# Hybrid SSD and S5 decoder block: S5 blocks in three parts with half projections between them, TensorE issued there in the written order

## The chip, the core and the metric

The kernel runs on one core of one Trainium2 chip. The metric is the device time of one execution in microseconds (us). The other cores do nothing. The inputs are float32, with a sequence of 512 tokens, 16 learned tokens ahead of it (528 in all) and a model width of 1024.

## What is computed

The reference, cut to what the change touches. The normalised input goes through one projection, whose columns are the gate `z`, the SSD input `xbc`, the step `dt` and the S5 input `u`. The S5 half is 64 groups of 16 channels, each with a complex state of 64 that runs over the whole sequence:

```python
proj = n @ w_in[layer]
z = proj[..., :o_xbc]
xbc = jax.nn.silu(_causal_depthwise_conv(proj[..., o_xbc:o_dt], conv_w[layer], conv_b[layer]))
u = proj[..., o_u:]
...
bu_re = jnp.einsum('blgh,gph->blgp', u, bb_re)
bu_im = jnp.einsum('blgh,gph->blgp', u, bb_im)
...
_, _, s_re, s_im = lax.associative_scan(combine, (a_re, a_im, bu_re, bu_im), axis=1)
y = (jnp.einsum('blgp,ghp->blgh', s_re, c_re.astype(f32))
     - jnp.einsum('blgp,ghp->blgh', s_im, c_im.astype(f32))
     + u * d_skip.astype(f32))
```

Behind that come a GLU on the S5 output, the chunked SSD on `xbc` with the gate `z`, the output projection and an MLP.

## The kernel before

Every large product is made of float32r parts: a weight is split into `whi` and `wlo` (lines 106 to 123), the input into `xhi` and `xlo`, and `mm_cols` (line 139) issues three matmuls for each of 8 slices of the contraction, 24 in all. The projection is made tile by tile of 128 columns. First come the 8 tiles of `u` (bank `pu`), which go to DRAM for the S5 blocks. The 12 tiles of `xbc` (bank `pxb`) are each made in two halves of 264 tokens, so there are 24 half projections of 24 matmuls; line 695 copies each out with ScalarE. The 8 tiles of `z` (bank `pz`) are made in one piece of 512 tokens, 24 matmuls each.

The S5 work is done in 8 blocks of 8 groups by `s5_block(b)`. In the order of its code a block has three parts, which the text calls A, B and C:

- A: VectorE makes powers of the state matrix (`qa`, `qb` at line 504, then `WB` and `CC` at line 509; there is one `WB` and there are two `CC`, used in turn). TensorE transposes `WB` (bank `pb`, line 519, two banks that ScalarE copies into `btr` and `bti`) and multiplies it with `CC` (bank `pk`, line 528). VectorE adds the skip term (line 530), and from `pk` the lag matrix `Tp` is laid out, by ScalarE copies for block 0 (line 535) and through DRAM for the others. ScalarE and VectorE make the cosine and sine tables `co` and `si` (lines 545 to 556; the second shows as `sni` in the profile).
- B: TensorE makes four banks `px` from `btr`, `bti` and the input `ub` (line 570). VectorE reads them in twelve instructions (lines 572 to 577), runs two scans (line 581) and six more instructions that give `sr` and, last, `si` (line 590).
- C: TensorE makes the bank `py` in 12 matmuls, in turn from `Tp`, `sr` and `si` (lines 594 to 597). ScalarE applies the Gelu (line 600, with a table load ahead of it) and the result goes to DRAM.

The banks `pb`, `pk`, `px` and `py` share four PSUM buffers, which are handed out in the order of the code. So each bank waits until the one four before it has been read. In the changed code the four `px` of block b + 1 come into the buffers of `pb` (two), `pk` and `py`: the first three follow A of block b + 1, the fourth waits for the Gelu of C of block b.

The convolution on `xbc` is 36 VectorE instructions (line 716, three for each of 12 tiles), each tile with a ScalarE instruction ahead (line 714) and a silu behind (line 718). A tile can be convolved as soon as its two halves are there. The step `dt` is worked out by small VectorE and ScalarE instructions (lines 608 to 672).

The code calls blocks 0 to 2, then the `dt` work, then blocks 3 to 7, then all `xbc` and `z` tiles. The order on the engines is another: a scheduler goes through the instructions with its own estimates of their times and gives each engine the ready instruction with the highest priority, earlier code first. It puts projection matmuls of later code wherever it thinks that TensorE would wait for the S5 blocks, and convolutions wherever it thinks that VectorE would. The order that it finds is then fixed, and each engine works its own list off from top to bottom.

Of the kernel before, what the change touches and what calls it, by code (L numbers as in the profile page):

```python
# [10 lines left out]
F32 = mybir.dt.float32  # L11
F32R = mybir.dt.float32r
I32 = mybir.dt.int32
AF = mybir.ActivationFunctionType
# [4 lines left out]
P = 128  # L19
SEQ = 512  # L20
NM = 16
L = SEQ + NM
LH = L // 2
DM = 1024
KD = DM // P
DFF = 4096
EPS = 1e-5
O_XBC = 1024
# [21 lines left out]
    return a.broadcast_to(shape)  # L50


@with_exitstack
def hybrid_block_kernel(ctx, tc, x, meta_tokens, g_mix, w_in, conv_w, conv_b, dt_bias, a_log, d_ssd,
                        g_ssd, lam_re, lam_im, log_step, b_re, b_im, c_re, c_im, d_s5, w_glu, b_glu,
                        g_s5, w_out, g_mlp, w_up, w_down, g_final, out, dbg=None):
    nc = tc.nc
    V, A, G, T = nc.vector, nc.scalar, nc.gpsimd, nc.tensor
    dma = nc.sync.dma_start
    dma2 = nc.sync.dma_start  # L60
    dbg = dbg or {}
# [8 lines left out]
    mid = ctx.enter_context(tc.tile_pool(name="mid", bufs=2))  # L70
# [8 lines left out]
    def bank(name, dt=F32):  # L79
        tag = KIND.get(name, "x")  # L80
        return ps.tile([P, 512], dt, tag=tag, name=name, bufs=TAGS[tag])

    def slot(name, shape, dt=F32):
        return big.tile(shape, dt, tag="slot", name=name)
# [24 lines left out]
    def split_weight(raw, lo_engine=None, ahead=AHEAD, room=None):  # L109
        with (tc.high_priority(offset=ahead) if ahead else nullcontext()):  # L110
            if room is None:
                hi = wp.tile(list(raw.shape), F32R, tag="hi", name="whi", bufs=3)
                lo = wp.tile(list(raw.shape), F32R, tag="lo", name="wlo", bufs=3)
            else:
                hi, lo = room("whi", list(raw.shape)), room("wlo", list(raw.shape))
            if lo_engine is V:
                A.copy(hi, raw)  # L117
                V.tensor_tensor(out=lo, in0=raw, in1=hi.bitcast(F32), op=ALU.subtract)  # L118
            else:

                A.mul(lo, raw, -1.0)
                G.dma_start(out=lo.bitcast(F32), in_=raw, accum_op=ALU.add)  # L122
                A.copy(hi, raw)  # L123
        return hi, lo

    def load_cols(w, c0, n=P, ahead=AHEAD):
        return load_weight(w[:, c0:c0 + n].rearrange("(k p) c -> p k c", p=P), KD, n, ahead)

    def w_cols(w, c0, n=P, lo_engine=None):
        return split_weight(load_cols(w, c0, n), lo_engine)  # L130
# [5 lines left out]
    def mm_cols(ps_out, w, x, m, tok):  # L136
        steps = [(k, a, b) for k in range(KD) for a, b in ((0, 0), (0, 1), (1, 0))]
        for n, (k, a, b) in enumerate(steps):
            T.matmul(ps_out, lhsT=w[a][:, k, 0:m], rhs=x[b][:, k, tok], start=(n == 0), stop=(n == len(steps) - 1))  # L139
# [101 lines left out]
    xx = (xhi, xlo)  # L241
    halves = (slice(0, LH), slice(LH, L))
# [250 lines left out]
    def s5_block(b):  # L493
        i = b % NB
# [45 lines left out]
        for t in range(TS5 if b else 0):  # L540
            dma2(out=Tp[i][96 - 32 * t:P - 32 * t, :, 32 * t:P],
                 in_=Kd[b][:, 0:P - 32 * t].rearrange("(j r) c -> r j c", j=4))
# [11 lines left out]
        A.activation(out=ta, in_=sh, func=AF.Square)  # L554
        A.activation(out=co, in_=ta, func=AF.Identity, scale=-2.0, bias=ones[:, 0:1])
        V.scalar_tensor_tensor(out=si, in0=sh, scalar=2.0, in1=ch, op0=ALU.mult, op1=ALU.mult)

        ub = s5.tile([P, 4, NC5], F32, tag="ub", name="ub", bufs=2)
        for t in range(TS5):
# [19 lines left out]
        for w in (wr, wi):  # L579
            w = w.rearrange("p j c -> p (j c)")  # L580
# [7 lines left out]
        V.tensor_tensor(out=tw, in0=wi, in1=co, op=ALU.mult)  # L588
        V.tensor_tensor(out=si_, in0=wr, in1=si, op=ALU.mult)
        V.tensor_tensor(out=si_, in0=si_, in1=tw, op=ALU.add)  # L590
        py = bank("py")
        for j in range(4):
            o = py[:, j * P:(j + 1) * P]
# [7 lines left out]
        for t in range(TS5):  # L601
            dma2(out=Yd[b][:, t, :].rearrange("(j g) c -> g j c", j=4), in_=yb[32 * t:32 * t + 32])

    for b in range(3):
        s5_block(b)


    pdt = bank("pdt")
    ND = 2 * NH
    T.transpose(pdt[0:NM, 0:ND], dtT[:, 0:NM], ident[:ND, :ND])  # L610
# [61 lines left out]
    dma2(out=eD, in_=erow)  # L672
    dump("dt", dt)

    for b in range(3, 8):
        s5_block(b)


    sz = slot("sz", [P, KD, SEQ])
    xcr = slot("xcr", [P, KD, L + 3])  # L680
    bcr = mid.tile([P, 4, L + 3], F32, tag="bcr", name="bcr", bufs=1)
    G.memset(xcr[:, :, 0:3], 0.0)
    G.memset(bcr[:, :, 0:3], 0.0)
    xc, bcT = xcr[:, :, 3:], bcr[:, :, 3:]
    order = [8, 9, 10, 11, 0, 1, 2, 3, 4, 5, 6, 7]

    def xbc_tile(f):
        return xcr[:, f] if f < 8 else bcr[:, f - 8]

    for f in order:  # L690
        w = w_cols(w_in[0], O_XBC + f * P)
        for i in range(2):
            pxb = bank("pxb")
            mm_cols(pxb[:, 0:LH], w, xx, P, halves[i])
            A.copy(xbc_tile(f)[:, 3 + LH * i:3 + LH * (i + 1)], pxb[:, 0:LH])  # L695

    for f in range(8):
        w = w_cols(w_in[0], f * P)
        pz = bank("pz")
        mm_cols(pz, w, xx, P, slice(NM, L))  # L700
        A.activation(out=sz[:, f], in_=pz, func=AF.Silu)


    yghi = slot("yghi", [P, KD, SEQ], F32R)
# [6 lines left out]
    for n, f in enumerate(order):  # L711
        raw = xbc_tile(f)
        acc = mid.tile([P, L], F32, tag="acc", name="acc")
        A.activation(out=acc, in_=raw[:, 0:L], func=AF.Identity, scale=col("cw", f), bias=col("cb", f))
        for k in (1, 2, 3):
            V.scalar_tensor_tensor(out=raw[:, 3:3 + L] if k == 3 else acc, in0=raw[:, k:k + L],
                                   scalar=col("cw", 12 * k + f), in1=acc, op0=ALU.mult, op1=ALU.add)
        last_silu = A.activation(out=raw[:, 3:3 + L], in_=raw[:, 3:3 + L], func=AF.Silu)
# [16 lines left out]
    for ch in range(NCH):  # L735
        n = NM if ch == 0 else P
# [15 lines left out]
        if ch > 0:  # L752
# [3 lines left out]
            for q in range(2):  # L756
                dma2(out=erep[64 * q:64 * q + 64],
                     in_=eD.rearrange("(r q) l -> q r l", q=2)[q, :, lt].partition_broadcast(64))
# [283 lines left out]
    class Cols:  # L1042
# [4 lines left out]
        def __init__(self, q, g):  # L1047
            self.q, self.g, self.b = q, g, {}
# [413 lines left out]
```

## Time and profile before

| | |
|---|---|
| time, median of 3 runs (lowest to highest) | 818.63 us (816.34 to 819.12) |
| profiled execution, its own time | 818.22 us |
| its span, first to last instruction | 816.5 us |
| mean granted TensorE clock | 0.992 |
| TensorE matmuls, busy | 774.8 us, 95% of the span |
| VectorE, busy | 625.4 us, 77% |
| ScalarE, busy | 496.3 us, 61% |

Times in the profile are counted from the start of the span. PE is TensorE, DVE is VectorE, ACT is ScalarE. A row of the timeline gives the start, the duration, the engine, the line, the operation, what it writes and reads, and in brackets how long the engine had waited and for whom. The duration of a matmul is longer than the distance to the next one, since matmuls overlap; the distance is what a row costs. A row of the windows gives a stretch of time and the busy time and instructions of each engine in it, then the granted TensorE clock. The S5 blocks and the `xbc` and `z` projections lie between 73.7 us and about 256 us.

### The profile page before, as it was taken

Reading aid. Unit: us, or ns where it says so; the run is one execution under the profiler, and the core shown is the slowest. Engines: PE = TensorE matmul, PEld = TensorE weight load, DVE = VectorE, ACT = ScalarE, POOL = GpSimd, SP = SyncE. Lnnn points to the kernel's source line nnn. Section 1 sums busy time; section 2 is a strip of 40 time slices with the busy share of each in tenths; the row PEclk is TensorE's granted clock in tenths of the full one; section 3 lists DMA queues with packets and bytes.
Section 4 is the critical chain, followed back from the end, with each engine's and each line's share of the span. In section 5 each row is a group of like instructions: output and inputs, shape, how many; then the busy total and the mean of one; then the engine's idle time right before and its main releaser. Section 6 shows DMA issues by size and latency. Waiting matters only on the chain. (4 is left out here: it accounts for less than half of the span.)

```text
span 816.5 us, 12922 instructions
## 1 busy us (share of the span) xinstructions
PE 774.8 (95%) x4943; PEld 682.5 (84%) x4943; DVE 625.4 (77%) x972; ACT 496.3 (61%) x782; POOL 75.9 (9%) x125
## 2 busy tenths in 40 slices
PE   6999899999999999989999998999999999999996
PEld 6999898998787778768888897878997899789975
DVE  4488898988775679769534589698779877987897
ACT  7578798988544663645213476654675466547665
POOL 3211000011000110010100000100010001000101
PEclk9999999999999999999999999999999999999999
DMA  8999675767754664353434118865485558654622
GB/s 242 178 218 212 149 166 138 176 141 171 160 147 126 180 129 127 87 148 130 156 104 154 54 52 263 191 160 160 130 180 154 159 136 172 180 161 112 116 51 104
DMA packets 129638, 121.90 MB, mean 149 GB/s; under 512 B 21836, under 2 KB 105720, under 8 KB 129576
## 3 DMA queue, kind: packets, MB, share of 16 engines
q1 hardware_dynamic: 121224, 90.66, 38.4%
q0 software_dynamic: 8352, 30.41, 20.5%
q8 instruction: 39, 0.64, 0.3%
q14 instruction: 23, 0.19, 0.1%
HBM read 83.76 MB, written 6.88 MB: 111 GB/s over the span
## 5 line engine op out<-in xcount | busy, mean ns | idle before, releaser
L1015 DVE TENSOR_TENSOR wlo<-quad,whi 128x1024 fp32r<-128x1024 f32 x40 | 49.0, 1224 | 36.3 <-ACT whi L1014 36.2
L1237 PE MATMUL u<-opC,whi 128*128 128x256 f32 x384 | 71.6, 288 | 3.9 <-DVE r L99 2.0
L1014 ACT CAST whi<-quad 128x1024 fp32r<-128x1024 f32 x40 | 41.9, 1048 | 54.6 <-DMA quad<-raw 18.6
L1278 PE MATMUL acc<-whi,al 128*128 128x512 f32 x160 | 63.4, 396 | 3.4 <-DVE al L1015 3.4
L1237 PEld LDWEIGHTS u<-opC,whi 128*128 128x128 f32 x384 | 60.6, 195 | 5.5 <-ACT whi L1014 2.5
L117 ACT CAST whi<-raw 128x1024 fp32r<-128x1024 f32 x31 | 32.4, 1044 | 52.1 <-PE acc L837 31.6
L118 DVE TENSOR_TENSOR wlo<-raw,whi 128x1024 fp32r<-128x1024 f32 x31 | 37.9, 1221 | 31.3 <-ACT whi L117 30.5
L1278 PE MATMUL acc<-whi,ah 128*128 128x512 f32 x160 | 59.5, 392 | 1.4 <-ACT ah L1014 1.4
L1278 PE MATMUL acc<-wlo,ah 128*128 128x512 f32 x160 | 60.4, 390 | 0.0
L139 PE MATMUL pxb<-xhi,whi 128*128 128x264 f32 x192 | 55.5, 289 | 1.6 <-ACT xcr L695 1.6
L139 PE MATMUL pxb<-xhi,wlo 128*128 128x264 f32 x192 | 56.1, 292 | 0.0
L139 PE MATMUL pxb<-xlo,whi 128*128 128x264 f32 x192 | 55.8, 291 | 0.0
L1237 PE MATMUL u<-opC,wlo 128*128 128x256 f32 x192 | 53.9, 287 | 0.0
L1014 ACT CAST whi<-bquad 128x1024 fp32r<-128x1024 f32 x34 | 35.7, 1049 | 29.9 <-PE acc L1278 20.7
L1237 PE MATMUL u<-opB,whi 128*128 128x256 f32 x256 | 47.2, 283 | 0.9 <-DVE opB L1015 0.6
L1237 PE MATMUL u<-opA,whi 128*128 128x256 f32 x256 | 46.7, 280 | 0.3 <-ACT whi L1014 0.3
L1015 DVE TENSOR_TENSOR wlo<-bquad,whi 128x1024 fp32r<-128x1024 f32 x34 | 41.5, 1222 | 3.2 <-ACT whi L1014 3.2
L1278 PEld LDWEIGHTS acc<-whi,al 128*128 128x128 f32 x160 | 30.0, 188 | 13.2 <-DVE al L1015 7.2
L1237 PEld LDWEIGHTS u<-opB,whi 128*128 128x128 f32 x256 | 39.5, 188 | 1.5 <-DVE opB L1015 0.8
L1237 PEld LDWEIGHTS u<-opA,whi 128*128 128x128 f32 x256 | 39.5, 188 | 0.8 <-ACT whi L1014 0.5
L122 POOL DMA_DIRECT2D wlo<-raw x26 | 22.3, 856 | 180.7 <-ACT xcr L695 63.4
L123 ACT CAST whi<-raw 128x1024 fp32r<-128x1024 f32 x26 | 27.1, 1043 | 18.8 <-PE pu L139 8.1
(435 smaller groups left out, 2441.5 us busy)
## 6 DMA issues: line engine op xcount, KB each, us to landing
raw<-in_w_in_dram SPq DMA_DIRECT2D x28, 512.0 KB, 4.2
wlo<-raw POOLq DMA_DIRECT2D x26, 512.0 KB, 5.1
raw<-in_w_up_dram SPq DMA_DIRECT2D x22, 512.0 KB, 4.7
raw<-in_w_glu_dram SPq DMA_DIRECT2D x16, 512.0 KB, 4.0
raw<-in_w_out_dram SPq DMA_DIRECT2D x16, 512.0 KB, 3.8
bquad<-in_w_down_dram SPq DMA_DIRECT2D x16, 512.0 KB, 3.7
quads<-in_w_down_dram SPq DMA_DIRECT2D x16, 512.0 KB, 4.3
bquad<-quads POOLq DMA_DIRECT2D x16, 512.0 KB, 5.2
```

The lines of the kernel that those rows point to most:

```text
L117: A.copy(hi, raw)
L118: V.tensor_tensor(out=lo, in0=raw, in1=hi.bitcast(F32), op=ALU.subtract)
L122: G.dma_start(out=lo.bitcast(F32), in_=raw, accum_op=ALU.add)
L123: A.copy(hi, raw)
L139: T.matmul(ps_out, lhsT=w[a][:, k, 0:m], rhs=x[b][:, k, tok], start=(n == 0), stop=(n == len(steps) - 1))
L1014: A.copy(hi, src)
L1015: last_low[:] = [V.tensor_tensor(out=lo, in0=src, in1=hi.bitcast(F32), op=ALU.subtract)]
L1237: T.matmul(pb[:, mm], lhsT=w[a][:, k, mm * P:(mm + 1) * P], rhs=x[:, b, k], start=(first and n == 0), stop=(n in (11, 23)), skip_group_che ...
L1278: T.matmul(banks[s], lhsT=at[x][:, g, j, s * P:(s + 1) * P], rhs=wt[y][:, j], start=(fresh and g == 0 and j == 0 and k == 0), stop=(g == 1 ...
```

## The change

`s5_block` becomes a generator that stops after A and after B. The projections become a generator too, which makes one half `xbc` tile (counted 1) or one whole `z` tile (counted 2) at a time. The driver calls them in turn: for block 2 and later it is B of block b, 2 counts of projection, A of block b + 1, 2 counts, C of block b, and then at once B of block b + 1. Blocks 0 and 1 have one half projection more behind C, and there are two halves between A and B of block 0. Two `z` tiles are left for the end.

TensorE's calls go through the wrapper `InOrder`. While `on` is set, each TensorE instruction is made to follow the one called before it, without a wait on the chip: it only binds the scheduler. The other engines' lists are still the scheduler's. In the lists of the changed kernel all TensorE rows stand under line 63, the wrapper's; lines of `s5_block` are 23 to 25 higher, and the convolution's is 768.

```diff
+class InOrder:
+    def __init__(self, tc, engine):
+        self.tc, self.engine, self.on, self.last = tc, engine, False, None
+
+    def __getattr__(self, name):
+        f = getattr(self.engine, name)
+
+        def issue(*args, **kwargs):
+            r = f(*args, **kwargs)
+            if self.on:
+                if self.last is not None:
+                    self.tc.add_manual_dep(
+                        r.ins, self.last.name,
+                        mybir.DependencyInfo(mybir.DependencyClass.NoSync, mybir.DependencyReason.DATA),
+                        reason="in order")
+                self.last = r.ins
+            return r
+
+        return issue
...
-    V, A, G, T = nc.vector, nc.scalar, nc.gpsimd, nc.tensor
+    V, A, G, T = nc.vector, nc.scalar, nc.gpsimd, InOrder(tc, nc.tensor)
...
         V.scalar_tensor_tensor(out=si, in0=sh, scalar=2.0, in1=ch, op0=ALU.mult, op1=ALU.mult)
+        yield
...
         V.tensor_tensor(out=si_, in0=si_, in1=tw, op=ALU.add)
+        yield
         py = bank("py")
...
-    for b in range(3):
-        s5_block(b)
...
+    def projections():
+        for f in order:
+            w = w_cols(w_in[0], O_XBC + f * P)
+            for i in range(2):
+                pxb = bank("pxb")
+                mm_cols(pxb[:, 0:LH], w, xx, P, halves[i])
+                A.copy(xbc_tile(f)[:, 3 + LH * i:3 + LH * (i + 1)], pxb[:, 0:LH])
+                yield 1
+        for f in range(8):
+            w = w_cols(w_in[0], f * P)
+            pz = bank("pz")
+            mm_cols(pz, w, xx, P, slice(NM, L))
+            A.activation(out=sz[:, f], in_=pz, func=AF.Silu)
+            yield 2
+
+    proj = projections()
+
+    def project(n):
+        while n > 0:
+            n -= next(proj, n)
+
+    T.on = True
+    blocks = [s5_block(b) for b in range(8)]
+    next(blocks[0])
+    project(2)
+    for b in range(2):
+        next(blocks[b])
+        project(2)
+        next(blocks[b + 1])
+        project(2)
+        next(blocks[b], None)
+        project(1)
+
+    T.on = False
     pdt = bank("pdt")
...
-    for b in range(3, 8):
-        s5_block(b)
...
+    T.on = True
+    for b in range(2, 8):
+        next(blocks[b])
+        project(2)
+        if b < 7:
+            next(blocks[b + 1])
+        project(2)
+        next(blocks[b], None)
+    T.on = False
+    project(40)
```

The order on TensorE from A of block 4 to B of block 4, before. `pk_1589` and the four `px_16..` are those of block 4, `py_1542` is C of block 3; the rows left out are `pxb` matmuls and the middle of `py_1542`.

```order
L528 MATMUL pk_1589<-CC0_983,WB_982 32x128 x8
L570 MATMUL px_1626<-ub_1618,btr_1580 128x132 x2
L570 MATMUL px_1629<-ub_1618,bti_1587 128x132 x2
L139 MATMUL pxb_2606<-xlo_92,whi_2575 128x264
...
L570 MATMUL px_1638<-ub_1618,btr_1580 128x132 x2
...
L595 MATMUL py_1542<-sr_1534,CC1_984 128x128
...
L597 MATMUL py_1542<-si_1535,CC1_984 128x128
L594 MATMUL py_1542<-ub_1499,Tp1_986 128x128
...
L597 MATMUL py_1542<-si_1535,CC1_984 128x128
L570 MATMUL px_1641<-ub_1618,bti_1587 128x132 x2
L139 MATMUL pxb_2724<-xhi_91,wlo_2694 128x264
```

The same place in the changed kernel. `pk_2106` and `px_2221` to `px_2236` are those of block 4, `py_2194` is C of block 3; left out are the rest of two half projections and the middle of `py_2194`.

```order
L63 MATMUL pk_2106<-CC0_983,WB_982 32x128 x8
L63 MATMUL pxb_2142<-xhi_91,whi_2137 128x264
...
L63 MATMUL py_2194<-ub_1976,Tp1_986 128x128
L63 MATMUL py_2194<-sr_2011,CC1_984 128x128
L63 MATMUL py_2194<-si_2012,CC1_984 128x128
...
L63 MATMUL py_2194<-si_2012,CC1_984 128x128
L63 MATMUL px_2221<-ub_2213,btr_2097 128x132 x2
L63 MATMUL px_2224<-ub_2213,bti_2104 128x132 x2
L63 MATMUL px_2233<-ub_2213,btr_2097 128x132 x2
L63 MATMUL px_2236<-ub_2213,bti_2104 128x132 x2
L63 MATMUL pxb_2263<-xhi_91,whi_2258 128x264
```

Before, three of block 4's four `px` stand ahead of C of block 3, and the matmuls on `sr` and `si` of that C stand apart, with `pxb` rows between them. Now exactly two half projections stand between A of block 4 and C of block 3, that C is one piece, and all of block 4's `px` come behind it.

The order on VectorE up to the last `si` of block 3, before. The rows at line 716 are the convolution.

```order
L581 SCALAR_TENSOR_TENSOR wi_1505<-decay_987,wi_1505 128x528
L716 SCALAR_TENSOR_TENSOR acc_3096<-xcr_2038,pcol_975,acc_3096 128x528
L572 TENSOR_TENSOR wr_1623<-px_1626,co_1610 128x264
L585 TENSOR_TENSOR tw_1506<-wi_1505,sni_1492 128x528
L716 SCALAR_TENSOR_TENSOR xcr_2038<-xcr_2038,pcol_975,acc_3096 128x528
L587 TENSOR_TENSOR sr_1534<-sr_1534,tw_1506 128x528
L556 SCALAR_TENSOR_TENSOR sni_1730<-sh_1727,ch_1728 128x528
L716 SCALAR_TENSOR_TENSOR acc_3102<-xcr_2038,pcol_975,acc_3102 128x528
L588 TENSOR_TENSOR tw_1506<-wi_1505,co_1491 128x528
L572 TENSOR_TENSOR wr_1623<-px_1638,co_1610 128x264
L716 SCALAR_TENSOR_TENSOR acc_3102<-xcr_2038,pcol_975,acc_3102 128x528
L590 TENSOR_TENSOR si_1535<-si_1535,tw_1506 128x528
```

The same in the changed kernel, up to the same instruction of block 3 (`si_2012`); the convolution's line is 768.

```order
L605 SCALAR_TENSOR_TENSOR wi_1982<-decay_987,wi_1982 128x528
L768 SCALAR_TENSOR_TENSOR acc_3090<-xcr_1016,pcol_975,acc_3090 128x528
L768 SCALAR_TENSOR_TENSOR xcr_1016<-xcr_1016,pcol_975,acc_3084 128x528
L609 TENSOR_TENSOR tw_1983<-wi_1982,sni_1891 128x528
L768 SCALAR_TENSOR_TENSOR acc_3090<-xcr_1016,pcol_975,acc_3090 128x528
L611 TENSOR_TENSOR sr_2011<-sr_2011,tw_1983 128x528
L579 SCALAR_TENSOR_TENSOR sni_2365<-sh_2362,ch_2363 128x528
L768 SCALAR_TENSOR_TENSOR xcr_1016<-xcr_1016,pcol_975,acc_3090 128x528
L768 SCALAR_TENSOR_TENSOR acc_3096<-xcr_1016,pcol_975,acc_3096 128x528
L612 TENSOR_TENSOR tw_1983<-wi_1982,co_1890 128x528
L768 SCALAR_TENSOR_TENSOR acc_3096<-xcr_1016,pcol_975,acc_3096 128x528
L614 TENSOR_TENSOR si_2012<-si_2012,tw_1983 128x528
```

Before, reads of block 4's first `px` banks (`wr_1623`) stand among the last instructions of block 3, with 13 convolution rows between the last `si` of block 2 and that of block 3. Now no `px` of block 4 is read there, and 19 convolution rows lie between the same two, 13 of them behind the first read of block 3's `px`. Over the eight blocks, the convolution rows that stand ahead of the last `si` of block b and behind that of block b - 1 were 16, 13 and 7 for b = 2, 3 and 4, and are now 7, 19, 5 and 5 for b = 2 to 5. Behind the last S5 block the list of TensorE is as before, but for C of block 7, which now stands among the last two `z` tiles and no longer among the first GLU matmuls.

More of the change, by code (lines that the diff above doesn't have):

```diff
@@ L602, in s5_block, with xbc_tile @@
             dma2(out=Yd[b][:, t, :].rearrange("(j g) c -> g j c", j=4), in_=yb[32 * t:32 * t + 32])
-    for b in range(3):
-        s5_block(b)
+    sz = slot("sz", [P, KD, SEQ])
+    xcr = slot("xcr", [P, KD, L + 3])
+    bcr = mid.tile([P, 4, L + 3], F32, tag="bcr", name="bcr", bufs=1)
+    G.memset(xcr[:, :, 0:3], 0.0)
+    G.memset(bcr[:, :, 0:3], 0.0)
+    xc, bcT = xcr[:, :, 3:], bcr[:, :, 3:]
+    order = [8, 9, 10, 11, 0, 1, 2, 3, 4, 5, 6, 7]
+    def xbc_tile(f):
+        return xcr[:, f] if f < 8 else bcr[:, f - 8]
+    def projections():
[28 more added lines that the diff above has]
+    T.on = False
     pdt = bank("pdt")
@@ L673, in hybrid_block_kernel @@
     dump("dt", dt)
-    for b in range(3, 8):
-        s5_block(b)
[L679 to L701, printed above, removed]
+    T.on = True
[8 more added lines that the diff above has]
+    project(40)
     yghi = slot("yghi", [P, KD, SEQ], F32R)
```

## The prediction

> **What bounds the kernel now.** I read the busy shares first, then the windows cut at the last `si` of each block, then TensorE's waits in the stage, then the rows that give prices.
>
> ```profile
> PE 774.8 (95%) x4943; PEld 682.5 (84%) x4943; DVE 625.4 (77%) x972; ACT 496.3 (61%) x782; POOL 75.9 (9%) x125
> ```
>
> TensorE bounds the whole. What matters is by how much, and who is next, in this stage. The windows give the stretch, its length, the busy time of TensorE, weight loads, VectorE, ScalarE and GpSimd, then the granted clock. The first runs from the last `si` of block 1 to that of block 2, and so on.
>
> ```profile
> 120.20:150.20 30.00, 28.43 (x246) 27.88 (x246) 27.04 (x48) 26.52 (x43) 2.56 (x3) 1.00 0.68 152
> 150.20:176.90 26.70, 24.05 (x198) 23.30 (x197) 25.11 (x46) 22.73 (x37) 2.54 (x3) 0.94 0.66 153
> 176.90:199.30 22.40, 22.40 (x153) 19.61 (x153) 21.02 (x38) 19.51 (x33) 2.55 (x3) 1.00 0.73 168
> 199.30:219.70 20.40, 18.83 (x120) 15.71 (x119) 16.67 (x32) 15.24 (x23) 1.70 (x2) 1.00 0.70 163
> 219.70:236.10 16.40, 16.40 (x108) 13.91 (x107) 12.09 (x24) 8.78 (x12) 1.70 (x2) 1.00 0.77 178
> ```
>
> VectorE is close to full in the first three: 27.04 of 30.00, 25.11 of 26.70, 21.02 of 22.40. The blocks that carry convolutions take longer, 30.0 and 26.7 us, and TensorE lives with it because it has more projection to do there. That stretch is elastic now. Its waits from 73 to 256 us (total, times, longest):
>
> ```profile
> PE pk L528 <- ACT btr L521: 2.4, 1, 2.4
> PE pxb L139 <- ACT xcr L695: 1.6, 1, 1.6
> PE py L594 <- DMA Tp<-Kd: 1.6, 1, 1.6
> PE px L570 <- ACT Tp L535: 1.3, 1, 1.3
> PE pb L519 <- ACT yb L600: 1.1, 2, 0.8
> PE py L594 <- DVE wi L575: 1.0, 1, 1.0
> PE px L570 <- ACT lag L538: 0.6, 1, 0.6
> PE pb L519 <- DVE tw L576: 0.5, 1, 0.5
> PE pv L139 <- ACT sz L701: 0.3, 1, 0.3
> ```
>
> They sum to 10.4 us; I count 10.3, the sum of the unrounded parts. The longest stands here:
>
> ```profile
> 164.71 0.76 PE L528 MATMUL pk<-CC,WB 128*32 128x128 f32 x16 [2.42 <-ACT btr L521]
> ```
>
> The window from 150.20, in which it lies, has a clock of 0.94: 26.70 x 0.06 = 1.6 us lost. So at most 10.3 + 1.6 = 11.9 us can be won here; the work itself is the same before and after.
>
> **TensorE's side of one block.** The distance of two starts is what a row costs.
>
> ```profile
> 73.71 1.09 PE L519 MATMUL pb<-ident,WB 128*128 128x128 f32 x8
> 75.78 0.64 PE L528 MATMUL pk<-CC,WB 128*32 128x128 f32 x16
> 79.87 0.61 PE L570 MATMUL px<-ub,btr 128*128 128x132 f32 x4
> 80.32 0.61 PE L570 MATMUL px<-ub,bti 128*128 128x132 f32 x4
> 102.09 0.39 PE L594 MATMUL py<-ub,Tp 128*128 128x128 f32 x2
> 102.76 0.39 PE L594 MATMUL py<-ub,Tp 128*128 128x128 f32 x2
> 160.04 0.28 PE L139 MATMUL pxb<-xhi,wlo 128*128 128x264 f32 x1
> 161.02 0.28 PE L139 MATMUL pxb<-xlo,whi 128*128 128x264 f32 x1
> 194.10 0.40 PE L139 MATMUL pz<-xhi,wlo 128*128 128x512 f32 x1
> 196.89 0.40 PE L139 MATMUL pz<-xhi,wlo 128*128 128x512 f32 x1
> ```
>
> A `px` costs 0.45, four 1.8. A costs 1.09 + 0.64 = 1.73. Three `py` matmuls lie between the two rows, 0.67, so `py` is 2.68. Eight `pxb` matmuls take 0.98, so a half projection of 24 takes 2.93; twelve `pz` take 2.79, a `z` tile 5.58. A block of the new order with four halves is therefore 1.8 + 1.73 + 2.68 + 4 x 2.93 = 17.9 us, one with two `z` tiles (blocks 5 to 7) 17.4. The new list fixes these numbers for every block, where the old one stretched to 30.
>
> **VectorE's side.** The convolution's price and the rows that stand between blocks:
>
> ```profile
> 148.85 0.77 DVE L716 SCALAR_TENSOR_TENSOR acc<-xcr,pcol,acc 128x528 f32<-128x528 f32 x1
> 149.53 0.70 DVE L590 TENSOR_TENSOR si<-si,tw 128x528 f32<-128x528 f32 x1
> 101.47 0.70 DVE L545 TENSOR_TENSOR ta<-th 128x528 f32<-128x528 f32 x1
> 226.25 1.39 DVE L509 TENSOR_TENSOR CC<-qa,qb 64x512 f32<-64x512 f32 x2 [3.18 <-PE py L597]
> ```
>
> The group of `qa` in the window from 150.20, with count, busy time and mean:
>
> ```profile
> L504 DVE TENSOR_TENSOR qa<-WW,PR 128x384 f32<-128x384 f32 (+1 forms) x2 | 1.2, 617 | 0.0
> ```
>
> A convolution row costs 0.68 (148.85 to 149.53). Taken from the windows, by the 16, 13 and 7 rows that the order counts there: 27.04 - 16 x 0.68 = 16.2, 25.11 - 13 x 0.68 = 16.3, 21.02 - 7 x 0.68 = 16.3, and 16.67 with none. So a block is 16.3 us of VectorE plus 0.68 for each convolution, and the model closes on four windows.
>
> VectorE's list is still the scheduler's, which has put 7, 19, 5 and 5 convolution rows into blocks 2 to 5. TensorE's C(b) needs the last `si` of block b, and nothing may pass it now; `px` of the next block, and so VectorE's next block, is queued behind it.
>
> - Block 3: VectorE needs 16.3 + 19 x 0.68 = 29.2 from the last `si` of block 2 to that of block 3; TensorE has 17.9. Wait **11.3**. VectorE has no pause there: the 6 convolutions, `ta` and `CC` behind `si` cover `py` and the first `px`.
> - Block 2 begins with VectorE waiting for `px`. Some 3.0 of the 16.3 lie ahead of that (`ta` 0.70 and `CC` 1.39, and `qa` with `qb`, some 0.5 each where rows overlap), so 13.3 + 7 x 0.68 + 0.45 = 18.5 against TensorE's 1.8 + 1.73 + 4 x 2.93 = 15.25. Wait 3.3.
> - Block 4: 16.3 + 5 x 0.68 = 19.7, and `WB`, which must now wait for `pk` of block 5, an operation that no row shows waiting so; between 0 and half of A, 0.9, I take the upper end, since few convolutions stand ahead of it here. 20.6 against 17.9: 2.7.
> - Block 5: the same, and 0.7 more since `CC` must wait for the whole of `py`, 2.68, which two convolutions and `ta` cover for 2.0; the row at 226.25 shows VectorE idle 3.18 for just this. 21.3 against 17.4: 3.9.
> - Block 1 has 2.9 more projection and no convolution: none.
>
> Two places are ScalarE's. Block 0, and the Gelu:
>
> ```profile
> 82.33 0.42 DVE L573 TENSOR_TENSOR tw<-px,sni 128x264 f32<-128x264 f32 x1
> 82.67 0.42 DVE L575 TENSOR_TENSOR wi<-px,co 128x264 f32<-128x264 f32 x1
> 86.03 0.27 ACT L629 ACTIVATE dt_e<-dt_e 128x80 f32<-128x80 f32 x1
> 86.32 0.38 ACT L695 COPY bcr<-pxb 128x264 f32<-128x264 f32 x1
> 86.33 0.20 DVE L632 TENSOR_SCALAR dt_z<-dt_e 128x80 f32<-128x80 f32 x1 [3.23 <-ACT dt_e L629]
> 100.70 0.70 DVE L590 TENSOR_TENSOR si<-si,tw 128x528 f32<-128x528 f32 x1
> 183.06 1.28 ACT L600 ACT_TABLE_LOAD   x1
> 184.35 0.60 ACT L600 ACTIVATE yb<-py 128x512 f32<-128x512 f32 x1
> ```
>
> - Block 0: VectorE's `dt` rows wait for ScalarE until 86.33, and all twelve `px` reads now stand behind them; three were ahead, at 0.34 each (82.33 to 82.67). One copy of 0.38 comes ahead of `dt_e`. So `si` comes near 100.70 + 3 x 0.34 + 0.38 = 102.1. TensorE is there at about 99.2 (79.87, + 1.8 + 5.86 + 1.73 + 5.86, + 2.1 for banks that `Tp` and `lag` hold, + two thirds of `py`). Wait 2.9, with the 2.1 sum 5.0.
> - The fourth `px` of the next block comes into the bank of `py` and waits for the Gelu: 1.28 + 0.60 + 0.1 = 2.0 behind `py`, of which the first three `px` cover 1.35. That is 0.65, and shows only in blocks 6 and 7, where VectorE is not the bound: 1.3.
>
> The Trainium skill, "ScalarE: Activation LUTs", section "What `ACT_TABLE_LOAD` costs", adds a drain of about 1.38 us to each load; here the Gelu starts 0.01 behind the 1.28, so the trace does not show it. By the page 2.8 would be added, 839.8.
>
> **The sum.** New waits 5.0 + 3.3 + 11.3 + 2.7 + 3.9 + 1.3 = 27.5; gone are 10.3 and the clock loss of 1.6. To that comes the clock behind the new waits. The only row is the 1.6 for a wait of 2.4; five new waits are that long or longer (blocks 0, 2, 3, 4, 5), so the bounds are 0 and 8.0. I take two, 3.2, since block 0 and 4 are only just over it. 27.5 + 3.2 - 10.3 - 1.6 = 18.8. The later stages begin that much later and are TensorE's, so nothing is given back. Against the profiled execution's 818.22 that is **837.0**; it lies 0.05% under the median, 818.63.
>
> The Trainium skill speaks here against the change too: "TensorE: Matmul & The Clock Gate", "Part 1: The HAM clock gate", has the clock halve when a window of about 3.4 us has been idle. The trace's loss behind 2.4 us is against that as a sharp limit. By the page only the waits of blocks 3 and 5 are long enough, and with block 3's loss alone the sum would be 835.4.
>
> **The rivals.**
>
> *VectorE keeps up, and waits vanish.* If VectorE reaches the last `si` of block 3 before TensorE, the written order only removes old waits: 818.2 - 11.9 = 806.3. For it: VectorE is idle for 2.96 of its first window's 30.00, and four `px` in a row feed it without the old pauses between them. It decides where 16.3 + n x 0.68 falls under 17.9, at two convolutions in a block, so 17 of the 19 would have to leave block 3. The order shows 13 behind the first `px` read, none of which can be early. 5%.
>
> *Only the big wait.* If blocks 2, 4 and 5 fit after all, waits are 5.0 + 11.3 + 1.3 = 17.6, and with no clock loss 818.2 + 17.6 - 11.9 = 823.9. Against it: the 16.3 closes on four windows. 14%.
>
> *ScalarE is late as well.*
>
> ```profile
> DVE acc L716 <- ACT acc L714: 3.9, 2, 2.9
> ```
>
> VectorE waited 3.9 for ScalarE's first product of a convolution. If block 3 with its six tiles repeats that and all five waits cost clock, 837.0 + 3.9 + 4.8 = 845.7. ScalarE was busy 26.52 of 30.00 in the window with 16 rows, so this is near. 18%.
>
> That the change doesn't do what it says is excluded by the order: four `px` stand behind each C, two halves between all parts.
>
> **How the numbers follow.** The forecast, 829 to 843, has 60%; with ScalarE late 18%, only the big wait 14%, VectorE keeps up 5%, something between these two that ends near the old time 3%. From 823 to 848 holds eight in ten and a little more. 0.3%, 2.5 us, is what a measurement can tell here. Faster 0.05, same 0.03, slower 0.92.
>
> **What would show it.** Right: a wait of about 11 us of `py` for `si` in block 3, waits of TensorE of 25 to 30 us in the stage, a clock under 1.00 behind them, VectorE full through blocks 2 and 3 and idle in 6 and 7, and the stage's end some 19 us later. Wrong: a wait in block 3 under 5 us, or C of block 3 released by something else than VectorE; or a stage as late as said whose time is won back behind it.

## The result

The changed kernel takes 841.93 us (median of 4 runs, 840.63 to 845.22) against 818.64 for the kernel before: 1.0286 times as long, 95% interval 1.0259 to 1.0314. The prediction said 837.0, with 823 to 848 as its range, for the reason that TensorE would wait for VectorE.

### The profile after

The profiled execution took 842.04 us, its span 840.3 us, 23.8 more than before. TensorE's busy time, from the page:

```profile
PE 780.8 (93%) x4943; PEld 688.2 (82%) x4943; DVE 626.0 (74%) x972; ACT 499.2 (59%) x784; POOL 75.3 (9%) x125
```

The same 4943 matmuls took 780.8 in place of 774.8 us, at a mean granted clock of 0.978 in place of 0.992: these 6.0 us are put down to the slower clock and are not waits. The first matmul of the bank `acc` (the output projection), which shows how late the whole is when the SSD and the GLU are done, of before and of after:

```profile
383.43 0.39 PE L837 MATMUL acc<-whi,y5hi 128*128 128x512 f32 x1
```

```profile
407.11 0.39 PE L63 MATMUL acc<-whi,y5hi 128*128 128x512 f32 x1
```

It is 23.7 us late there, and the end is 23.8 us late: all is lost before it, and nothing is given back.

The windows of the changed kernel, from the last `si` of each block to the next, blocks 2 to 6. A row gives the stretch and its length, the busy time of TensorE, weight loads, VectorE, ScalarE and GpSimd, and then the granted clock, the share of DMA and its GB/s:

```profile
123.07:151.70 28.63, 24.86 (x215) 23.68 (x213) 21.87 (x42) 23.89 (x39) 2.55 (x3) 1.00 0.71 168
151.70:181.49 29.79, 21.59 (x160) 20.74 (x160) 29.19 (x51) 24.25 (x41) 2.54 (x3) 0.79 0.56 120
181.49:202.49 21.00, 18.64 (x150) 18.08 (x151) 19.82 (x37) 12.72 (x24) 0.85 (x1) 0.90 0.33 74
202.49:228.00 25.51, 20.23 (x123) 17.20 (x122) 20.05 (x38) 19.03 (x27) 1.70 (x2) 0.87 0.51 115
228.00:242.74 14.74, 14.16 (x98) 11.88 (x97) 12.00 (x24) 8.52 (x11) 1.70 (x2) 1.00 0.68 160
```

Block 3 is the second row: VectorE is busy for 29.19 of its 29.79 us, TensorE for 21.59, at a clock of 0.79. TensorE's waits from 73 to 290 us (total, times, longest):

```profile
PE py L63 <- DVE si L614: 9.1, 4, 3.9
PE px L63 <- ACT yb L625: 7.7, 4, 5.3
PE py L63 <- DVE sr L611: 6.8, 3, 5.1
PE px L63 <- ACT Tp L558: 1.6, 1, 1.6
PE pv L63 <- ACT yghi L761: 1.3, 2, 1.0
PE pv L63 <- ACT sz L653: 0.3, 1, 0.3
```

These are 26.8 us; the same count, to 285 us, was 10.5 before. Of the old list only the waits for `Tp` and `sz` are left; `py` waits for `sr` and `si` (15.9 us) and the fourth `px` for the Gelu, `yb` (7.7). So the 23.8 us are 26.8 - 10.5 = 16.3 of waits and 7.5 of other things, 6.0 of which is the clock in the busy time. This counts where TensorE's time went and not yet what caused it: where VectorE sets the length of a block, a slow clock only fills time that would else be a wait.

The largest wait is the forecast one, C of block 3. TensorE's rows there:

```profile
178.37 0.80 PE L63 MATMUL py<-sr,CC 128*128 128x128 f32 x2 [5.12 <-DVE sr L611]
182.26 0.80 PE L63 MATMUL py<-si,CC 128*128 128x128 f32 x2 [3.10 <-DVE si L614]
182.85 0.64 PE L63 MATMUL py<-ub,Tp 128*128 128x128 f32 x2
183.28 0.64 PE L63 MATMUL py<-sr,CC 128*128 128x128 f32 x2
...
185.78 0.39 PE L63 MATMUL py<-sr,CC 128*128 128x128 f32 x2
186.00 0.39 PE L63 MATMUL py<-si,CC 128*128 128x128 f32 x2
```

Two waits of 8.2 us in all. Behind them a row of two matmuls costs 0.43 (182.85 to 183.28); at the end of the same `py` it costs 0.22 (185.78 to 186.00): half the clock for some 3 us.

The second largest was not forecast in this size. TensorE's row and ScalarE's rows ahead of it, in block 5:

```profile
212.70 1.25 PE L63 MATMUL px<-ub,bti 128*128 128x132 f32 x4 [5.28 <-ACT yb L625]
```

```profile
205.59 1.28 ACT L574 ACT_TABLE_LOAD   x1
206.88 0.64 ACT L574 ACTIVATE sh<-ta 128x528 f32<-128x528 f32 x1
207.44 0.81 ACT L766 ACTIVATE acc<-xcr,pcol 128x528 f32<-128x528 f32 x1
208.26 1.28 ACT L770 ACT_TABLE_LOAD   x1
209.56 0.65 ACT L770 ACTIVATE xcr<-xcr 128x528 f32<-128x528 f32 x1
210.11 0.63 ACT L575 ACTIVATE ta<-ta 128x528 f32<-128x528 f32 x1
210.75 1.28 ACT L625 ACT_TABLE_LOAD   x1
212.05 0.60 ACT L625 ACTIVATE yb<-py 128x512 f32<-128x512 f32 x1
```

`py` was done near 206.1 (a VectorE row that waits for it starts at 206.11). The Gelu starts 6 us later, since ScalarE's list has two rows for the cosine and sine tables (`sh`, `ta`), a first product and a silu of the convolution ahead of it, with two table loads more. The fourth `px` waits for all of that, because it comes into the bank of `py`.

### The profile page after: what moved, and what is told of

Read it like the earlier page. It is cut to its first block, busy times and chain, and to the rows that moved or that the text cites. A ratio compares the mean times of both kernels' runs of the same rounds, so it can differ in the third digit from the quotient of the medians.

```text
span 840.3 us, 12923 instructions
## 1 busy us (share of the span) xinstructions
PE 780.8 (93%) x4943; PEld 688.2 (82%) x4943; DVE 626.0 (74%) x972; ACT 499.2 (59%) x784; POOL 75.3 (9%) x125
## 5 line engine op out<-in xcount | busy, mean ns | idle before, releaser
L63 PE MATMUL acc<-whi,al 128*128 128x512 f32 (+1 forms) x200 | 76.6, 386 | 3.3 <-DVE al L1067 3.3
L63 PE MATMUL acc<-whi,ah 128*128 128x512 f32 (+1 forms) x200 | 72.9, 384 | 1.4 <-ACT ah L1066 1.4
L63 PE MATMUL acc<-wlo,ah 128*128 128x512 f32 (+1 forms) x200 | 73.8, 383 | 0.0
L63 PEld LDWEIGHTS acc<-whi,al 128*128 128x128 f32 x200 | 37.6, 188 | 14.0 <-DVE al L1067 7.2
L63 PEld LDWEIGHTS acc<-whi,ah 128*128 128x128 f32 x200 | 37.4, 189 | 9.7 <-ACT ah L1066 2.6
L63 PEld LDWEIGHTS acc<-wlo,ah 128*128 128x128 f32 x200 | 37.7, 189 | 7.0
```

The costliest lines, as they stand in the source:

```text
L63: r = f(*args, **kwargs)
```

## The experiments

The theory: with TensorE's order fixed, each block gives it a fixed amount of work, the fill, and where the convolutions make VectorE's block longer than that, TensorE waits. The first rival: it is the new order of the code, with its rotation of the banks. The second: it is ScalarE and the wait for the Gelu. The third: it is the slow clock behind the waits. Ratios are to the kernel before on the same chip, with 95% intervals.

### Without the binding

```diff
-    T.on = True
     blocks = [s5_block(b) for b in range(8)]
...
-    T.on = True
     for b in range(2, 8):
```

> The code in three parts as in the changed kernel, but TensorE's instructions are not bound to the written order. If the binding is what costs (VectorE falls behind and TensorE has nothing it may pass forward), the time comes back to 815 to 828 us and TensorE's waits in the stage fall from 25 to under 15 us. If the new order of the code costs, with its rotation of the banks, it stays over 835 us and the fourth px still waits some 7 us for the Gelu.

818.98 us, ratio 1.0012 (0.9996 to 1.0028). TensorE's waits from 73 to 285 us are 8.6, and the largest is 3.7, in the GLU. The order of the code and its rotation of banks cost nothing that can be measured as long as the scheduler may move TensorE's rows; the 23 us come with the binding. The scheduler moved the convolutions too, to 19 rows in block 4 and 17 in block 5, and TensorE got longer blocks there, as before. The window of the unbound kernel's block 4:

```profile
158.50:192.27 33.77, 32.65 (x235) 29.58 (x234) 30.02 (x52) 29.66 (x45) 2.96 (x4) 1.00 0.60 137
```

With 19 rows VectorE is busy for 30.02 us, as in block 3 of the bound kernel, and TensorE has 32.65 us of work beside it where the bound order gives it 17.9.

### Without VectorE's convolution, after and before

In both kernels, the same three lines are left out. What is computed changes: the silu takes the projection as it is.

```diff
-        for k in (1, 2, 3):
-            V.scalar_tensor_tensor(out=raw[:, 3:3 + L] if k == 3 else acc, in0=raw[:, k:k + L],
-                                   scalar=col("cw", 12 * k + f), in1=acc, op0=ALU.mult, op1=ALU.add)
```

> The changed kernel without the 36 convolution rows of VectorE; ScalarE's rows of the convolution stay. If VectorE's convolutions make the waits, block 3 shrinks from 29.8 us to about 18.5, the waits for sr and si in blocks 2 and 3 (12.8 us) vanish with the half clock behind them, and the time is near 822 us. If ScalarE and the banks make them, the px waits for the Gelu stay at 7 us and the time stays over 832 us.

> The kernel before without the 36 convolution rows of VectorE: the yardstick for the changed kernel without them. If the convolutions make the loss, this one lies 3 to 10 us under that one, where with them the distance is 23. If they don't, the distance stays near 20. By itself it should gain little, 3 to 8 us, since before TensorE waited for VectorE hardly at all.

823.48 us after and 824.12 before, one run each. The distance of 23 us between the two is gone, as the theory has it. The waits of `py` for `sr` and `si` fall from 15.9 us to 2.8, block 0's, but 17.1 us of waits are left in all, 5.2 of them for the Gelu: the convolutions on VectorE are not the whole of the loss, and this kernel is still 5.6 us above the kernel before with its convolutions (817.85). Two numbers were not as expected. The kernel before did not gain but came out 6 us slower than with the convolutions: less work on VectorE makes the scheduler find another order, with other waits (4.8 us for the load of `ub`, 2.9 in the GLU). And block 3 of the changed kernel without convolutions is not 18.5 us:

```profile
143.43:168.91 25.48, 20.03 (x160) 19.11 (x159) 16.49 (x33) 25.31 (x43) 2.55 (x3) 0.87 0.49 113
```

VectorE has 16.49 us, the 16.3 of the sum without convolutions, and ScalarE is busy for 25.31 of 25.48. So beneath VectorE's 29.19 us ScalarE is the next bound of this block.

### A bank of its own for `py`

```diff
-            "pq2": "q", "pdt": "q", "pa": "q", "par": "q"}
+            "pq2": "q", "pdt": "q", "pa": "q", "par": "q", "pyq": "q"}
...
-        py = bank("py")
+        py = bank("pyq" if b > 1 else "py")
```

> The changed kernel with py of block 2 and later in a PSUM buffer of its own, so that no px waits for the Gelu. If that wait is a cause by itself, its 7.5 us (1.6, 5.3 and 0.7) and the half clock behind the 5.3 go: about 833 us. If VectorE is the bound beneath it, blocks 4 and 5 end only where VectorE's own work lets them, at 20.6 and 21.3 us against 21.0 and 25.5 now: about 837 us, with waits for si in their place. Blocks 2 and 3 stay as they are in both.

834.84 us, ratio 1.0213 (1.0193 to 1.0232), between the two and 7.1 us under the changed kernel (6.0 by the ratios). The waits for the Gelu are gone. The window of block 5 and the waits of `py` of this kernel:

```profile
200.93:221.48 20.55, 18.16 (x116) 15.06 (x114) 19.78 (x38) 20.31 (x28) 1.70 (x2) 1.00 0.65 148
```

```profile
PE pyq L63 <- DVE si L614: 8.9, 4, 3.9
PE pyq L63 <- DVE sr L611: 7.0, 3, 5.5
```

Block 5 falls from 25.51 to 20.55, near the 21.3 that the sum gives for VectorE, and `py` waits 2.8 us for `sr` and `si` there in place of 5.7 before it. So about half of that wait was VectorE's beneath, and half a cause by itself. The waits of blocks 2 and 3 are nearly as they were (4.2 and 8.6 us for 4.5 and 8.2).

### The convolution spread

```diff
-        for k in (1, 2, 3):
-            V.scalar_tensor_tensor(out=raw[:, 3:3 + L] if k == 3 else acc, in0=raw[:, k:k + L],
-                                   scalar=col("cw", 12 * k + f), in1=acc, op0=ALU.mult, op1=ALU.add)
+        with tc.issue_after(ends[1 + n // 2].ins):
+            for k in (1, 2, 3):
+                V.scalar_tensor_tensor(out=raw[:, 3:3 + L] if k == 3 else acc, in0=raw[:, k:k + L],
+                                       scalar=col("cw", 12 * k + f), in1=acc, op0=ALU.mult, op1=ALU.add)
```

`ends` holds the last `si` instruction of each block.

> The changed kernel with the convolution spread on VectorE: six rows in each of blocks 2 to 7 (tile n is held behind the last si of block 1 + n // 2), where it was 7, 19, 5 and 5. If VectorE's sum of work against the fill that is fixed makes the loss, each block now has 16.3 + 6 x 0.68 = 20.4 us of VectorE against 17.9 or 17.4 of TensorE: waits of 2.5 to 5 us in six blocks, 25 us in all as before; only the half clock gets less, so about 836 us. If the heap of 19 rows in block 3 alone makes it, the time falls under 828 us.

826.74 us, ratio 1.0096 (1.0064 to 1.0128), 15 us faster than the changed kernel (16 by the ratios). That is 9 us better than expected, and the mistake was in the expectation. Blocks 4, 6 and 7 of this kernel:

```profile
172.18:192.71 20.53, 18.37 (x160) 17.62 (x160) 20.37 (x38) 19.62 (x32) 1.70 (x2) 1.00 0.65 143
213.24:229.37 16.13, 15.55 (x103) 12.98 (x102) 15.98 (x30) 12.58 (x18) 1.70 (x2) 1.00 0.74 166
229.37:245.23 15.86, 15.07 (x86) 12.93 (x85) 14.82 (x26) 9.35 (x11) 1.50 (x2) 1.00 0.61 141
```

In blocks 3 to 5 VectorE sets the length, 20.5 to 21.0 us for the sum's 20.4. But of A of a later block VectorE has only the last `CC` left to make in block 6 and nothing in block 7: block 6 took 12.00 us of it in the changed kernel and 12.09 before. Six convolutions fit in there without a wait of TensorE for VectorE, and 16.3 was the wrong base for these two: 16.13 and 15.86 us in place of twice 20.4 are the 9 us. So the time, though it is under 828, doesn't show that a heap of 19 rows is a cause by itself; the rows were moved to where there was room.

### More work for TensorE in the waits

```diff
         project(2)
+        again({2: 1, 3: 3}.get(b, 0))
         next(blocks[b], None)
```

`again(n)` repeats n half projections into a bank that nobody reads. The scheduler put 17 and 10 convolution rows into blocks 3 and 4.

> The changed kernel with four half projections more, repeats into a bank that nobody reads: one ahead of C of block 2, three ahead of C of block 3, 11.7 us of work for TensorE. VectorE's list has 17 rows in block 3 and 10 in block 4 in place of 19 and 5. If TensorE truly waits there for VectorE, the work fits into the waits and costs nothing, and what was lost by the half clock behind the waits (py of block 3 took 4.1 us in place of 2.7) comes back: 837 to 842 us. If TensorE's own work sets the time, it is 853 us.

841.80 us, ratio 1.0268 (1.0242 to 1.0294): 11.7 us of additional matmuls cost nothing. TensorE's waits to 285 us fall from 26.8 to 15.5. Blocks 3 and 4:

```profile
151.26:179.69 28.43, 26.94 (x232) 26.31 (x232) 27.84 (x50) 20.72 (x35) 1.70 (x2) 1.00 0.47 110
179.69:203.37 23.68, 18.88 (x163) 17.75 (x161) 23.18 (x41) 20.88 (x35) 2.54 (x3) 0.99 0.55 124
```

VectorE's sum is 16.3 + 17 x 0.68 = 27.9 and 16.3 + 10 x 0.68 = 23.1; it was busy 27.84 and 23.18. The clock in block 3 is 1.00 in place of 0.79, and the block is 1.4 us shorter, which is what two convolution rows less are worth (2 x 0.68). The clock that was lost inside a block that VectorE sets did not cost time, and a wait filled with useless work is no gain. This answers the third rival for block 3; behind block 0 no run tests the clock alone.

### More useful work in the early blocks

```diff
     for b in range(2, 8):
         next(blocks[b])
-        project(2)
+        project(3 if b < 6 else 2)
```

In a part of the edit that is not shown, `project` carries over what a whole `z` tile takes too much.

> The changed kernel with the fill alone evened out, five counts of projection in blocks 2 to 5; the banks as in the changed kernel and the convolution left to the scheduler, which puts 8, 16 and 12 rows into blocks 2, 3 and 4. By VectorE's sum block 3 is 16.3 + 16 x 0.68 = 27.2 us against TensorE's 20.9, block 4 is 24.5 against 20.9, the others fit: waits of about 6.4 + 3.6 + 1 beside block 0's 4.4 and some 2 for the Gelu, 17 us, and about 832 us. If more fill is enough by itself, waits fall under 10 us and the time under 822 us, as with all three edits together.

824.34 us, ratio 1.0089 (1.0065 to 1.0112); 832 was expected from the sum. TensorE's waits fall to 15.3 us. Block 3 took 27.62 us for the sum's 27.2, with waits of 5.4 in it for the 6.4 expected. Block 4 took 23.55 with only 0.76 of wait, for the Gelu, where 3.6 were expected. No gap is longer than 3.4 us, and the mean clock is 0.991 where the changed kernel had 0.978: most of the slow clock, which the expectation left as it was, went with the long waits.

### The edits together, and C one block later

The first of these has the evened fill, the spread convolution and the bank of its own together.

> The changed kernel's order with the fill evened out: five counts of projection in blocks 2 to 5 and four in 6 and 7, py in a bank of its own, six convolution rows in each of blocks 2 to 7; px of block b + 1 still behind C of block b. TensorE has 20.9 us in blocks 0 to 5 against VectorE's 20.4, and 17.9 against 20.4 in the last two. If balance is the cause, the waits fall to those of block 0 (5 us), some 3 in each of the last two and little else: 815 to 824 us. If px behind C is what costs, waits of 2 to 4 us stay in every block: over 830 us.

812.82 us, ratio 0.9924 (0.9900 to 0.9947): faster than both kernels. By the ratios the fill alone was worth 16 us against the changed kernel, the spread 16 and the bank 6; together they give 30, since they take from the same waits. Its windows of blocks 3 and 4, and its waits:

```profile
150.94:172.08 21.14, 20.38 (x180) 20.02 (x181) 20.57 (x38) 19.21 (x34) 2.54 (x3) 1.00 0.71 149
172.08:190.24 18.16, 18.01 (x139) 16.35 (x138) 18.01 (x32) 15.84 (x22) 1.70 (x2) 1.00 0.79 188
```

```profile
PE pyq L63 <- DVE si L616: 2.2, 2, 1.2
PE px L63 <- ACT Tp L560: 1.7, 1, 1.7
PE py L63 <- DVE si L616: 1.7, 1, 1.7
PE py L63 <- DVE sr L613: 1.1, 1, 1.1
```

Both engines are full, and 6.7 us of waits are left, 4.5 of them in block 0. VectorE's 18.01 us in block 4 are less than the sum's 20.4, but block 5 has 23.03: the two together are 41.0 for the sum's 40.8.

The second has the same spread, the bank of its own and another written order: `px` of block b + 1 ahead of C of block b, with five counts of projection per block. Blocks 0 and 1, whose lines are not shown, are called in the same way.

```diff
+    project(1)
+    next(blocks[2])
+    project(2)
     for b in range(2, 8):
         next(blocks[b])
+        project(1)
+        next(blocks[b - 1], None)
         project(2)
         if b < 7:
             next(blocks[b + 1])
-        project(2)
-        next(blocks[b], None)
+            project(2)
+    project(4)
+    next(blocks[7], None)
```

> Bound to a written order too, but another: px of block b + 1 ahead of C of block b, so that VectorE goes from block to block without a pause, and C has a half projection and the px between it and the wait; py in a bank of its own, five counts of projection per block and six convolution rows in each of blocks 2 to 7. TensorE then has 6.2 + 5 x 2.93 = 20.9 us per block and VectorE 20.4. If the balance of the two is the cause, the waits in the stage fall under 12 us and the time is 808 to 820 us, at or below the kernel before. If a fixed order as such costs, it stays over 828 us.

813.29 us, ratio 0.9942 (0.9918 to 0.9965), with 8.3 us of waits, none of them of `py` for `sr` or `si`. The two intervals overlap: with this balance no difference is seen between C ahead of the next `px` and behind it.

### The `dt` rows behind block 0

```diff
-    V.tensor_scalar(out=z2, in0=e, scalar1=2.0, scalar2=None, op0=ALU.add)
+    with tc.issue_after(ends[0].ins):
+        V.tensor_scalar(out=z2, in0=e, scalar1=2.0, scalar2=None, op0=ALU.add)
```

By itself on the changed kernel:

> The changed kernel with VectorE's rows of dt held behind the last si of block 0; TensorE's list is word for word the same. If those rows with their wait for ScalarE make block 0's 2.8 us of waits, these go, with the half clock behind them, and nothing later takes them back, since TensorE is the bound in block 1: 837 to 839 us. If VectorE only moves the 4 us of dt rows into block 1 and is late there, it stays at 841 to 843 us.

838.06 us, ratio 1.0248 (1.0219 to 1.0277). The median is in the first range that was expected, but the interval overlaps the changed kernel's. Block 0's waits for `sr` and `si` are gone, and its last `si` starts at 99.02 and no longer at 101.91. But the profiled execution, the slowest of the four at 843.03, lost it again in block 2. The row of VectorE's waits there, of the changed kernel and of this one:

```profile
DVE acc L768 <- ACT acc L766: 1.6, 1, 1.6
```

```profile
DVE acc L771 <- ACT acc L769: 3.7, 1, 3.7
```

ScalarE's first product of the convolution writes into a buffer from which a row of the `dt` work is stored to DRAM, and by the profile it waited 4.2 us for that store in the changed kernel and 6.4 in this one. The store landed at nearly the same time in both, so an earlier block 0 only waits longer. The two runs at 835.9 suggest that it need not be so; they have no trace, and this stays open.

With the three other edits:

> The kernel with the evened fill, the spread convolution and the bank of its own, and the dt rows held behind the last si of block 0 as well. If block 0's wait is a cost by itself, 809 us, 3 to 4 us under that kernel's 812.8; if the dt rows come to lie in the way of block 1, no change from it.

808.66 us, ratio 0.9898 (0.9870 to 0.9926), 1.0% faster than the kernel before, the lowest of all. 4.6 us of waits are left, none of them block 0's for `sr` and `si`. The interval overlaps that of the kernel without this edit (0.9900 to 0.9947), so by the times its gain of some 2 to 4 us is not shown.

Last, this kernel without the binding:

> The kernel with all four edits (evened fill, six convolution rows in each of blocks 2 to 7, py in a bank of its own, dt rows behind block 0), TensorE's instructions not bound to the written order. If the gain of 1% over the kernel before comes from VectorE's even load and the free bank, it stays without the binding: 806 to 811 us. If the written order with its five counts of fill per block is needed for it, the scheduler's own placing gives 814 to 822 us, as it gave 819 for the unbound three-part code.

820.66 us, ratio 1.0038 (1.0012 to 1.0065). The scheduler's own order, with 9, 9, 6, 6 and 6 convolution rows in blocks 3 to 7, is 12 us slower than the written one (11 by the ratios). Its waits to 285 us are 10.4 for 4.6. From 240 to 388 us, the windows of the bound and of the unbound kernel:

```profile
240.00:388.00 148.00, 143.08 (x767) 113.06 (x767) 113.54 (x179) 76.21 (x147) 8.89 (x8) 1.00 0.47 141
```

```profile
240.00:388.00 148.00, 137.64 (x725) 106.61 (x724) 107.61 (x175) 72.94 (x142) 11.05 (x8) 0.95 0.47 121
```

It has 5 us less of TensorE there, at a clock of 0.95, since its last S5 block ends 13 us later (the last `si` at 256.5 and at 243.4) and the GLU behind it begins with waits. The same binding that costs 23 us with four counts of fill per block gains some 12 with five, a spread convolution, a bank of its own for `py` and the `dt` rows later.

## Why the prediction was right

**What can be won.** 11.9 us were put as the most that this stage can give back. The best kernel here gains 8.4 (817.03 to 808.66).

**TensorE's and VectorE's sums.** These held. A block of VectorE as 16.3 + 0.68 per convolution gave 29.2 for block 3 (measured 29.8), 20.6 for block 4 (21.0), and in the experiments 27.9, 23.1, 20.4 and, without convolutions, 16.3 (busy 27.84, 23.18, 20.37, 16.49). It fails for blocks 6 and 7, where block 6 shows a base of 12, which no term of the prediction used.

**The waits, block by block,** forecast and measured:

| | forecast | measured |
|---|---|---|
| block 0 | 5.0 | 4.4: `px` 1.6, `sr` 1.1, `si` 1.7 |
| block 2 | 3.3 | 4.5: VectorE waited 1.6 for a first product that waited for a store |
| block 3 | 11.3 | 8.2: TensorE's 17.9 us became 21.6, at a clock of 0.79, most of it behind block 2's wait |
| block 4 | 2.7 | 1.6, for the Gelu, not for `si` |
| block 5 | 3.9 | 5.7: 5.3 for the Gelu, 0.4 for `si` |
| blocks 6, 7 | 1.3 | 0.8, for the Gelu |

The sum is 25.2 for 27.5. That these are so near is luck in part: the waits for `sr` and `si` are 15.9 us where 24.1 were put, and those for the Gelu 7.7 where 1.3 were. Block 0 has luck in it too. Its terms add up to 99.0 and not 99.2; TensorE came there at 99.41, since its first `px` stood at 82.00 and not at 79.87, and since one row of `py` stands ahead of the wait and not two thirds of it.

The wait for the Gelu was forecast as a mechanism, with 0.65; the step that failed is that only its own table load and 0.60 lie between `py` and its end. ScalarE's list, on which the change has no hold, had four more instructions and two more loads ahead of it in block 5, so that one wait was 5.28 us, and in a block that was put under VectorE alone.

**What is gone.** Of the 10.3 us before, little is left, as said.

**The miss of 5 us.** By TensorE's time it looks like the clock: 3.2 us, two losses, were put in. Against 17.2 us of net waits forecast, 16.3 were measured; the rest, 7.5 us, is against 3.2 - 1.6 = 1.6. The bound of 8.0 for the new losses was near: the busy time gives 6.0 + 1.6 = 7.6, and 1.5 us more are in neither waits nor busy time. But the two terms are not independent, as the sum has them. In block 3 the clock that was lost came out of the wait, 8.2 + 3.7 for the 11.3 forecast, and with the clock back the block was shorter only by its two convolution rows less.

The lengths of the blocks that VectorE should set say more: 29.2, 20.6 and 21.3 us were forecast for blocks 3 to 5, and 29.79, 21.00 and 25.51 measured. Block 5 alone is 4.2 us longer, and there it is the Gelu: with a bank of its own it takes 20.55 us, and the whole is 6 to 7 us faster where the sum has 1.3 for the Gelu. So the term that was mis-sized is in the first place the wait for the Gelu. Smaller ones add to it: block 2's wait was 1.2 us longer, and the GLU's `pv` waits are 1.6 us for 0.5 before, which the sum has not. How much the clock cost by itself, behind block 0 above all, no run shows.

The forecast's other figure, 835.4, counts one clock loss although the sentence before it names two waits as long enough, blocks 3 and 5; with two it is 837.0 again.

**The clock.** The windows behind the waits of blocks 0, 2, 3 and 5 and behind the single one of block 4:

```profile
102.00:105.00 3.00, 2.33 (x15) 2.33 (x16) 1.59 (x5) 2.98 (x5) 0.20 (x1) 0.80 0.71 199
152.40:158.00 5.60, 5.55 (x26) 5.55 (x27) 5.09 (x8) 4.63 (x7) 0.73 (x1) 0.50 0.51 96
178.00:186.00 8.00, 4.54 (x20) 4.24 (x21) 7.63 (x12) 4.26 (x7) 0.00 (x0) 0.52 0.50 116
212.00:216.00 4.00, 3.30 (x10) 2.82 (x11) 2.04 (x6) 3.91 (x6) 0.00 (x0) 0.50 0.61 155
189.00:192.00 3.00, 2.67 (x22) 2.67 (x23) 3.00 (x9) 0.28 (x1) 0.00 (x0) 1.00 0.37 87
```

The clock was low behind four waits, not two, and behind the longer ones it was near half over 4 to 8 us, a larger loss than the 1.6 us of the one row before. The Trainium skill's rule of a half clock after an idle window of about 3.4 us ("TensorE: Matmul & The Clock Gate", "Part 1: The HAM clock gate") agrees with the 0.50 to 0.52 behind the waits of 3.9, 5.1 and 5.3 us. The traces do not show it as a limit for a single wait: block 0's two, 1.1 and 1.7 us with two matmuls between, were followed by 0.80 as well, the single 2.42 us of the kernel before by 0.52 from 165 to 168, while the 1.6 of block 4 left 1.00.

**The rivals.** That VectorE keeps up did not happen, nor that block 3's wait stands alone. ScalarE as an additional blocker came true in part: VectorE waited 2.4 us for first products where 3.9 were put, and the Gelu's wait is ScalarE's too. 841.9 lies between the forecast and that rival's 845.7.

## What to carry to other kernels

A written order fixes how much work the bound engine has between two dependencies, so its fill must be counted against the other engine's sum, block by block; with four counts per block it cost 23 us here; with five, an even convolution, a free bank and the `dt` rows moved it came out 8 us under the kernel before. An order on one engine was worth little here while the lists of the engines that feed it are still another's choice. The single waits of 2.4 us and more that were looked at were followed by about half the clock, those of 1.7 and less were not, which speaks for many short waits where TensorE is the bound behind them; inside a block that VectorE set, the lost clock cost nothing, and no run here tests the advice alone.

## What was not expected of the hardware

A slow clock followed two waits of 1.1 and 1.7 us that two matmuls parted (0.80 over the 3 us from 102), as well as single waits of 3.9 us and more. In the kernel with the spread convolution a single wait of 3.37 us was followed by 0.51 from 152.3 to 155.6, waits of 0.67 and 1.49 us, parted in the same way and 2.2 us together, by 0.50 from 193.5 to 196.6, and the single wait of 2.42 us in the kernel before by 0.52 from 165 to 168. Near 2 us it goes both ways: a wait of 2.09 us in the unbound last kernel was followed by 0.50 from 233.3 to 236.0, one of 2.08 in the kernel with more fill by 1.00 from 152.5 to 156.0. And taking 36 rows, 22 us of busy time, away from VectorE made the kernel before not faster but some 6 us slower in a single run (824.12 for 817.85), with other waits in the new order that the scheduler found. So leaving work out shows the cost of that work only between two kernels that are treated alike.
